# The loads at three stage boundaries in another order, and the down-projection's weight sums on the vector engine alone

## The chip, the cores and the metric

The kernel runs on one core of one Trainium2 chip. The metric is the device time of one execution in microseconds. Five engines work side by side, each through its own list of instructions in order: PE (matrix multiplication), DVE (vector), ACT (scalar), POOL (GpSimd) and SP (which here only issues DMAs). A DMA that SP or POOL issues runs on the 16 DMA engines, and what is queued behind it on its issuer goes on at once unless it has a wait of its own.

## The reference

One decoder layer over 512 tokens with a model width of 2048 and an inner width of 5632, all in float32: sliding-window attention, and then a gated MLP with a causal convolution of width 3 over the positions.

```python
def conv_ffn(h, w_up, conv_w, w_down):
    u = h @ w_up                                             # 512x2048 @ 2048x11264
    up = jnp.pad(u, ((0, 0), (CONV_WIDTH - 1, 0), (0, 0)))
    c = conv_w[0] * up[:, 0:S]
    for j in range(1, CONV_WIDTH):
        c = c + conv_w[j] * up[:, j:j + S]
    gate, val = jnp.split(c, 2, axis=-1)
    return (jax.nn.silu(gate) * val) @ w_down                # 512x5632 @ 5632x2048

h = rms_norm(x, norm_g[0, 0])
m = swa_sink_attention(h, swa_w_in[0], swa_w_out[0], swa_sinks[0], rel_bias_table)
x = x + rms_norm(m, norm_g[0, 1])
h = rms_norm(x, norm_g[0, 2])
x = x + rms_norm(conv_ffn(h, ffn_w_up[0], ffn_conv[0], ffn_w_down[0]), norm_g[0, 3])
```

## The kernel before

Float32 accuracy comes from splitting each operand into a high and a low part: ACT copies the block into the high part (`wh`, line 64), DVE subtracts that from the block for the low part (`wl`, line 65), and each product is three matmuls (`prod`, line 83 records them): high by high, high by low, low by high. Matmuls are issued in program order, and so are the DMAs that go through `in_turn` (line 139, on SP). The order of all other instructions on DVE, ACT and POOL is set by the compiler's scheduler from its own model of time.

The stages are: projections and attention, the output projection, the up-projection, the down-projection. The up-projection works by pairs: for one f, a block of 128 gate columns and 128 value columns for all 512 tokens. f = 0 to 3 are computed in other ways; `up_by_tokens(3)` is the last of these, and its activation forms are computed in a space named `keepers`. Then 40 calls of `up_pair(f)`, f = 4 to 43, follow, counted here as pair 0 to 39. A pair uses seven products in place of eight (a Strassen form): it loads four weight blocks of 512 KB (`b11`, `b21`, `b12`, `b22`, tile `bw`, six buffers), makes four sums of them on DVE (lines 697, 704, 708, 711), splits seven blocks, and multiplies each by a form of the activations, 24 matmuls of 128x256 for one product. DVE also combines the results (lines 715, 717, 719). `gate(f)` then does the convolution (lines 583 to 585) and the gate (590, 592), and stores a tile of `hd` in DRAM through POOL.

The down-projection also uses seven products, of 22 steps over kp, with matmuls of 128x512. Four of them need sums of weight blocks, which are computed ahead and kept in DRAM as `td`: `weight_sums(kp)` loads four blocks of `wdn` of 512 KB into four `ts` tiles, adds on DVE (line 147, four adds) and stores four results through POOL (line 148). `queue_sums(kp)` does the same without DVE: four loads on SP and then four accumulating DMAs on POOL (line 157) and the stores (line 160). The groups kp = 0 to 5 are done within the output projection. The other 16 are done beside the pairs: at every fifth pair (i%5 == 0) a `weight_sums` is begun ahead of the pair's own loads, its adds come in and behind the next pair, and then a `queue_sums` follows. The `ts` tiles (pool `tsu`, four buffers) lie in the space that `keepers` held.

When the last group is done, at i = 36, `tsu` is closed, a tile `hq10` for 16 steps of the first down product's activations is opened in its place, and four fetches of 512 KB from `hd` are issued on SP. The down stage reads its blocks into `raw`, by turns from two pools of two buffers, `wraw` (which the pairs also use) and `wraw2`, which is opened when the up stage is over. `coming` is the list of later fetches; one is issued with every second step of kp.

Of the kernel before, what the change touches and what calls it, by code (L numbers as in the profile page):

```python
# [11 lines left out]
F32 = mybir.dt.float32  # L12
# [6 lines left out]
P = 128  # L19
# [16 lines left out]
NP = NF // 2  # L36
HALF = S // 2
# [4 lines left out]
def trunk(ctx, tc, xT, x, grow, table, onehot, masked, sinks, conv,  # L42
          wkv, wq, wo, wup, wdn, out):
    nc = tc.nc
    pool = lambda name, bufs, **kw: tc.tile_pool(name=name, bufs=bufs, **kw)

    const = ctx.enter_context(pool("const", 1))
    wraw = ctx.enter_context(pool("wraw", 2))
# [8 lines left out]
    def bank(i):  # L57
        return ps.tile([P, 512], F32, name=f"b{i}", bufs=1)
# [4 lines left out]
    def split(hi, lo, src):  # L63
        nc.scalar.activation(hi, src, AF.Copy)  # L64
        nc.vector.tensor_tensor(lo, src, hi.bitcast(F32), ALU.subtract)  # L65

    def halves():
        p = ring["slots"][ring["next"] % len(ring["slots"])]
        ring["next"] += 1
        return p.tile([P, 1024], F32R, name="wh"), p.tile([P, 1024], F32R, name="wl")  # L70
# [67 lines left out]
    def in_turn(o, i):  # L138
        tc.keep_in_program_order(nc.sync.dma_start(o, i))  # L139

    def weight_sums(kp, sums, paced=False):
        t = [sums.tile([P, 1024], F32, name="ts") for _ in range(4)]
        for q in (0, 2, 1, 3):
            (in_turn if paced else nc.gpsimd.dma_start)(t[q], wdn[4 * kp + q])
        yield
        for q, o in ((2, 0), (0, 1), (1, 2), (3, 1)):
            nc.vector.tensor_tensor(t[q], t[q], t[o], ALU.add)
            nc.gpsimd.dma_start(td[kp, :, q, :], t[q])
            yield

    def queue_sums(kp, sums):
        t = [sums.tile([P, 1024], F32, name="ts") for _ in range(4)]
        for q in (2, 0, 1, 3):
            in_turn(t[q], wdn[4 * kp + q])

        def add(q, o):
            nc.gpsimd.dma_start(t[q], o, accum_op=ALU.add)

        def store(q):
            nc.gpsimd.dma_start(td[kp, :, q, :], t[q])  # L160

        add(2, wdn[4 * kp])
        add(0, wdn[4 * kp + 1])
        store(2)
        add(1, t[2])
        store(0)
        add(3, t[1])
        store(1)
        store(3)

    def step(g, n=1):
        for _ in range(n):
            next(g, None)

    with ExitStack() as att:
# [10 lines left out]
        with ExitStack() as ph:  # L186
# [26 lines left out]
            for kt in range(KT):  # L213
                if kt == 0:
                    for h in range(2):
# [3 lines left out]
                        if h == 0:  # L219
                            w = halves()  # L220
                            raw = wraw.tile([P, 1024], F32, name="raw")
# [241 lines left out]
    with ExitStack() as op:  # L463
        sums = op.enter_context(pool("tso", 4))
# [5 lines left out]
        g1 = gp.tile([P, D], F32, name="g1")  # L470
# [63 lines left out]
        for b, bk in enumerate((2, 5, 6, 7)):  # L534
            o = bank(bk)
            for kt in range(KT):
# [3 lines left out]
                if b < 2:  # L540
                    if kt == 0:
                        g = weight_sums(4 + b, sums)
# [23 lines left out]
    batches = [(g, min(g + GB, NP)) for g in range(0, NP, GB)]  # L566
    hq = {}

    def fetch(m, par, g0, g1):
        t, k0 = next((t, k) for t, k, k1 in hq[m, par] if k <= g0 < k1)  # L570
        in_turn(t[:, g0 - k0:g1 - k0, :], hd[m, par, :, g0:g1, :])

    with ExitStack() as us:
# [14 lines left out]
        def gate(f, o):  # L588
            cg = conv_half(o[0], f, 0)
            nc.scalar.activation(cg, cg, AF.Silu)  # L590
            cv = conv_half(o[1], f, 1)
            nc.vector.tensor_tensor(cv, cg, cv, ALU.mult)  # L592
            kp, par = divmod(f, 2)
            nc.gpsimd.dma_start(hd[:, par, :, kp, :].rearrange("m p t -> p m t"),  # L594
                              cv.rearrange("p (m t) -> p m t", m=2))
# [71 lines left out]
        tsu = ExitStack()  # L667
        sums = tsu.enter_context(pool("tsu", 4, side="right"))

        def block(f, r, c):  # L670
            t = bw.tile([P, 1024], F32, name="bw")
            in_turn(t, wup[4 * f + 2 * c + r])
            return t

        def form(t):
            w = halves()
            split(*w, t)
            return w

        def times(o, n, w, fresh):  # L680
            o3 = o[:, :HALF].rearrange("p (a b) -> p a b", a=2)
            a = forms[n]
            for k in range(8):
                prod(o3, cols(w, k), tuple(v[:, :, k, :] for v in a), fresh and k == 0, k == 7, not fresh)

        def shot(o, name):
            t = un.tile([P, HALF], F32, name=name)
            nc.scalar.activation(t, o[:, :HALF], AF.Copy)  # L688
            return t

        def up_pair(f, g):
            X, Y, Z = (bank(k) for k in ((0, 1, 6), (3, 4, 7))[f % 2])
            ug = un.tile([P, S], F32, name="ug", bufs=2)
            uv = un.tile([P, S], F32, name="uv", bufs=2)
            b11, b21 = block(f, 0, 0), block(f, 1, 0)
            t = wraw.tile([P, 1024], F32, name="raw")
            nc.vector.tensor_tensor(t, b11, b21, ALU.add)  # L697
            times(X, 2, form(t), True)
            s1 = shot(X, "s1")
            step(g)  # L700
            b12 = block(f, 0, 1)
            times(Z, 7, form(b12), True)
            s7 = shot(Z, "s7")
            nc.vector.tensor_tensor(t, t, b12, ALU.add)
            times(X, 5, form(t), False)
            s2 = shot(X, "s2")
            step(g)
            nc.vector.tensor_tensor(b11, b11, b12, ALU.add)  # L708
            times(Z, 6, form(b11), False)
            b22 = block(f, 1, 1)  # L710
            nc.vector.tensor_tensor(t, t, b22, ALU.add)
            times(X, 3, form(t), False)
            s3 = shot(X, "s3")
            step(g)
            nc.vector.tensor_tensor(ug[:, :HALF], Z[:, :HALF], s2, ALU.subtract)
            times(Y, 1, form(b21), True)
            nc.vector.tensor_tensor(uv[:, :HALF], s3, s7, ALU.subtract)
            times(X, 4, form(b22), False)
            nc.vector.tensor_tensor(ug[:, HALF:], s1, Y[:, :HALF], ALU.subtract)
            nc.scalar.activation(uv[:, HALF:], X[:, :HALF], AF.Copy, scale=-1.0)  # L720
            gate(f, (ug, uv))

        kp = 6
        for f in range(4, NF):
            i = f - 4
            if i % 5 == 0 and kp < NP:
                work = weight_sums(kp, sums, True)
                step(work)
                kp += 1
            up_pair(f, work if i % 5 == 1 else iter(()))  # L730
            if i % 5 == 1:
                step(work)
            if i % 5 == 1 and kp < NP:
                queue_sums(kp, sums)
                kp += 1
            if kp == NP and tsu:
                tsu.close()
                tsu = None
                early = ctx.enter_context(pool("early", 1, side="right"))
                hq[1, 0] = [(early.tile([P, 16, HALF], F32, name="hq10"), 0, 16)]  # L740
                for g0, g1 in batches[:4]:
                    fetch(1, 0, g0, g1)


    acts.close()
# [3 lines left out]
    y = acc.tile([P, NT, D], F32, name="y")  # L749
    g3 = acc.tile([P, D], F32, name="g3")  # L750
    rest = ctx.enter_context(pool("rest", 1))
    hq[1, 0].append((rest.tile([P, NP - 16, HALF], F32, name="hq10b"), 16, NP))
    raws = (wraw, ctx.enter_context(pool("wraw2", 2)))
    for m, par in ((0, 1), (1, 1)):
        hq[m, par] = [(rest.tile([P, NP, HALF], F32, name=f"hq{m}{par}"), 0, NP)]
    small = ctx.enter_context(pool("small3", 4))
    last = ctx.enter_context(ExitStack())
    hq[0, 0] = [(last.enter_context(pool("hq00", 1)).tile([P, NP, HALF], F32, name="hq00"), 0, NP)]
    coming = [(1, 0, *g) for g in batches[4:]] + [(*q, *g) for q in ((0, 0), (0, 1), (1, 1)) for g in batches]
    nc.scalar.dma_start(g3, grow[2:3, :].to_broadcast([P, D]))  # L760

    XB, ZB = (3, 4, 6, 7), (0, 1, 2, 5)
# [16 lines left out]
        return hi, lo  # L779

    def weight_form(src, kp):
        raw = raws[kp % 2].tile([P, 1024], F32, name="raw")
        table, q = src
        in_turn(raw, td[kp, :, q, :] if table else wdn[4 * kp + q])
        hi, lo = halves()
        split(hi, lo, raw)
        return hi, lo
# [5 lines left out]
    def product(o, form, src, fresh, tail=0):  # L793
        kept = []
        for g0, g1 in batches:
            af = act_form(*form, g0, g1)
            for kp in range(g0, g1):
                wf = weight_form(src, kp)
                if coming and kp % 2 == 0:
                    fetch(*coming.pop(0))  # L800
                if kp >= NP - tail:
                    kept.append((kp, af, g0, wf))
                    continue
                for t in range(2):
                    for e in range(2):
                        multiply(o, kp, af, g0, wf, t, e, fresh)
        return kept
# [13 lines left out]
    sums = {}  # L821
# [23 lines left out]
    product(z_, (a11, a21, 1), (0, 1), True)  # L845
    keep(x_, 1, 0)
    product(x_, (a12, a21, 1), (1, 1), False)
    keep(z_, 0, 1)
    product(z_, (a12, a11, -1), (1, 0), False)
# [93 lines left out]
```

## Time and profile before

| | us |
|---|---|
| median of 3 runs | 1907.91 (1906.57 to 1908.58) |
| the profiled execution | 1905.1 |
| its span | 1903.1 |
| PE busy | 1859.6 (98%) |
| DVE busy | 1456.7 (77%) |
| ACT busy | 982.3 (52%) |
| POOL busy | 124.0 (7%) |

The profile is of one execution, and its times count from the start of the span. An instruction's row gives its start, its duration, the engine and line, the tile that it writes and those that it reads, and in brackets the time that the engine stood idle before it and what released it. `DMA bw<-in_wup` as a releaser is the landing of that transfer. The starts of successive matmuls lie closer together than their durations, since matmuls are pipelined. The granted clock is the share of TensorE's full clock, where 1.00 is 2.4 GHz and 0.50 is 1.2 GHz.

### The profile page before, as it was taken

Reading aid. Unit: us, or ns where it says so; the run is one execution under the profiler, and the core shown is the slowest. Engines: PE = TensorE matmul, PEld = TensorE weight load, DVE = VectorE, ACT = ScalarE, POOL = GpSimd, SP = SyncE. Lnnn points to the kernel's source line nnn. Section 1 sums busy time; section 2 is a strip of 40 time slices with the busy share of each in tenths; the row PEclk is TensorE's granted clock in tenths of the full one; section 3 lists DMA queues with packets and bytes.
Section 4 is the critical chain, followed back from the end, with each engine's and each line's share of the span. In section 5 each row is a group of like instructions: output and inputs, shape, how many; then the busy total and the mean of one; then the engine's idle time right before and its main releaser. Section 6 shows DMA issues by size and latency. Waiting matters only on the chain.

```text
span 1903.1 us, 30165 instructions
## 1 busy us (share of the span) xinstructions
PE 1859.6 (98%) x11822; PEld 1688.7 (89%) x11822; DVE 1456.7 (77%) x2047; ACT 982.3 (52%) x1566; POOL 124.0 (7%) x196
## 2 busy tenths in 40 slices
PE   9999999999999599999999999999998999999998
PEld 7888888888899599999999999999997888888886
DVE  5468888754787689898989898989875666666875
ACT  6357777622443355555555555555544555545553
POOL 0000000012100111101010101010100000000000
PEclk9999999999999799999999999999998999999999
DMA  9533234499641767667585758575652876575673
GB/s 306 157 98 97 93 119 144 149 348 335 245 166 61 263 190 255 210 228 232 200 249 211 244 202 266 193 242 206 200 208 90 326 275 212 176 245 187 245 249 113
DMA packets 112397, 392.02 MB, mean 206 GB/s; under 512 B 13216, under 2 KB 15488, under 8 KB 110336
## 3 DMA queue, kind: packets, MB, share of 16 engines
q1 hardware_dynamic: 83968, 293.86, 44.8%
q0 software_dynamic: 24256, 87.04, 14.4%
q10 hardware_dynamic: 4032, 9.21, 1.5%
q8 instruction: 92, 1.51, 0.3%
q14 instruction: 49, 0.40, 0.1%
HBM read 309.29 MB, written 72.39 MB: 201 GB/s over the span
## 4 chain that ended last, share of the span: by engine, by line
PE 62%; issue 2%; DMA 1%; DVE 1%; ACT 0%; POOL 0%; DVEq 0%; SPq 0%; ACTq 0%; POOLq 0%
PE b L83 62%; DMA bw<-in_wup 0%; DMA raw<-td 0%; DVE wl L65 0%; DMA hd<-c 0%; DVE x L839 0%; POOL hd L594 0%; DVE raw L697 0%; DVE bw L708 0%; ACT wh L64 0%; ACT junk L828 0%; DVE y L830 0%; DVEq L939 0%; DVE c L592 0%; SPq L139 0%
## 5 line engine op out<-in xcount | busy, mean ns | idle before, releaser
L64 ACT ACTIVATE wh<-raw 128x1024 fp32r<-128x1024 f32 (+1 forms) x371 | 388.9, 1056 | 485.0 <-PE b L83 275.8
L65 DVE TENSOR_TENSOR wl<-raw,wh 128x1024 fp32r<-128x1024 f32 (+1 forms) x371 | 449.6, 1219 | 212.0 <-ACT wh L64 210.6
L83 PE MATMUL b<-ah,wh 128*128 128x256 f32 (+1 forms) x1824 | 563.6, 309 | 18.5 <-ACT wh L64 18.5
L83 PE MATMUL b<-ah,wl 128*128 128x256 f32 (+1 forms) x1824 | 557.2, 305 | 2.6 <-DVE wl L65 2.6
L83 PE MATMUL b<-al,wh 128*128 128x256 f32 (+1 forms) x1824 | 556.3, 305 | 0.4 <-DVE al L65 0.4
L83 PEld LDWEIGHTS b<-ah,wh 128*128 128x128 f32 x1824 | 351.1, 192 | 31.0 <-ACT wh L64 20.4
L83 PEld LDWEIGHTS b<-ah,wl 128*128 128x128 f32 x1824 | 350.6, 192 | 18.3 <-DVE wl L65 3.6
L83 PEld LDWEIGHTS b<-al,wh 128*128 128x128 f32 x1824 | 351.2, 193 | 10.9 <-DVE al L65 0.6
L83 PE MATMUL b<-wh 128*128 128x512 f32 x616 | 241.2, 392 | 6.8 <-ACT wh L64 6.8
L64 ACT ACTIVATE wh<-bw 128x1024 fp32r<-128x1024 f32 x160 | 169.1, 1059 | 147.8 <-PE b L83 144.1
L83 PE MATMUL b<-wl,wh 128*128 128x512 f32 x616 | 241.4, 392 | 1.7 <-DVE wl L65 1.7
L83 PE MATMUL b<-wh,wl 128*128 128x512 f32 x616 | 241.1, 391 | 0.0
L65 DVE TENSOR_TENSOR wl<-bw,wh 128x1024 fp32r<-128x1024 f32 x160 | 194.2, 1218 | 7.6 <-ACT wh L64 6.7
L83 PEld LDWEIGHTS b<-wh 128*128 128x128 f32 x616 | 116.4, 189 | 32.2 <-ACT wh L64 7.8
L83 PEld LDWEIGHTS b<-wl,wh 128*128 128x128 f32 x616 | 116.5, 189 | 26.7 <-DVE wl L65 2.6
L83 PEld LDWEIGHTS b<-wh,wl 128*128 128x128 f32 x616 | 116.5, 189 | 24.1
L83 PE MATMUL b<-wh,ah 128*128 128x512 f32 x320 | 126.5, 395 | 0.0
L83 PE MATMUL b<-wh,al 128*128 128x512 f32 x320 | 124.8, 390 | 0.0
L83 PE MATMUL b<-wl,ah 128*128 128x512 f32 x320 | 124.6, 389 | 0.0
L83 PE MATMUL b<-f6h,wh 128*128 128x256 f32 x320 | 91.4, 286 | 2.6 <-ACT s L688 2.6
L83 PE MATMUL b<-f6l,wh 128*128 128x256 f32 x320 | 91.3, 285 | 0.0
L83 PE MATMUL b<-f6h,wl 128*128 128x256 f32 x320 | 91.2, 285 | 0.0
(165 smaller groups left out, 3031.8 us busy)
## 6 DMA issues: line engine op xcount, KB each, us to landing
bw<-in_wup SPq DMA_DIRECT2D x160, 512.0 KB, 4.4
td<-ts POOLq DMA_DIRECT2D x88, 512.0 KB, 5.4
raw<-td SPq DMA_DIRECT2D x88, 512.0 KB, 5.0
raw<-in_wdn SPq DMA_DIRECT2D x66, 512.0 KB, 4.5
ts<-in_wdn SPq DMA_DIRECT2D x64, 512.0 KB, 6.2
ts<-in_wdn POOLq DMA_DIRECT2D x40, 512.0 KB, 8.4
raw<-in_wq SPq DMA_DIRECT2D x32, 512.0 KB, 3.5
raw<-in_wo SPq DMA_DIRECT2D x32, 512.0 KB, 5.0
```

The lines of the kernel that those rows point to most:

```text
L64: nc.scalar.activation(hi, src, AF.Copy)
L65: nc.vector.tensor_tensor(lo, src, hi.bitcast(F32), ALU.subtract)
L83: tc.keep_in_program_order(nc.tensor.matmul(o, l, r, start=start, stop=stop, skip_group_check=more))
```

## The change

All 16 groups beside the pairs now go through `weight_sums`; `queue_sums` stays in the file and is not called. A group's four loads are issued ahead of the loads of the pairs 1, 3, 5, 7, 9, 11, 13, 16, 18, ..., 28, 31 and 33, and its adds are recorded within and behind the pair after it. Pair 0's loads therefore come first on SP. `tsu` is closed behind the whole loop; `hq10` holds 8 steps in place of 16, two fetches follow it, and `wraw2` is opened beside it. In the down stage the four raw buffers are used in turn, and the fetches that were left over are placed behind raws number 3 to 6, the later ones at every second step as before.

```diff
--- before.py
+++ after.py
@@ -723,23 +723,22 @@
         kp = 6
         for f in range(4, NF):
             i = f - 4
-            if i % 5 == 0 and kp < NP:
+            if i % 15 in (1, 3, 5, 7, 9, 11, 13) and kp < NP:
                 work = weight_sums(kp, sums, True)
                 step(work)
                 kp += 1
-            up_pair(f, work if i % 5 == 1 else iter(()))
-            if i % 5 == 1:
-                step(work)
-            if i % 5 == 1 and kp < NP:
-                queue_sums(kp, sums)
-                kp += 1
-            if kp == NP and tsu:
-                tsu.close()
-                tsu = None
-                early = ctx.enter_context(pool("early", 1, side="right"))
-                hq[1, 0] = [(early.tile([P, 16, HALF], F32, name="hq10"), 0, 16)]
-                for g0, g1 in batches[:4]:
-                    fetch(1, 0, g0, g1)
+                up_pair(f, iter(()))
+            else:
+                up_pair(f, work if i else iter(()))
+                if i:
+                    step(work)
+        assert kp == NP
+        tsu.close()
+        early = ctx.enter_context(pool("early", 1, side="right"))
+        hq[1, 0] = [(early.tile([P, 8, HALF], F32, name="hq10"), 0, 8)]
+        wraw2 = ctx.enter_context(pool("wraw2", 2, side="right"))
+        for g0, g1 in batches[:2]:
+            fetch(1, 0, g0, g1)
 
 
     acts.close()
@@ -749,14 +748,14 @@
     y = acc.tile([P, NT, D], F32, name="y")
     g3 = acc.tile([P, D], F32, name="g3")
     rest = ctx.enter_context(pool("rest", 1))
-    hq[1, 0].append((rest.tile([P, NP - 16, HALF], F32, name="hq10b"), 16, NP))
-    raws = (wraw, ctx.enter_context(pool("wraw2", 2)))
+    hq[1, 0].append((rest.tile([P, NP - 8, HALF], F32, name="hq10b"), 8, NP))
+    raws = {"pools": (wraw, wraw, wraw2, wraw2), "next": 0}
     for m, par in ((0, 1), (1, 1)):
         hq[m, par] = [(rest.tile([P, NP, HALF], F32, name=f"hq{m}{par}"), 0, NP)]
     small = ctx.enter_context(pool("small3", 4))
     last = ctx.enter_context(ExitStack())
     hq[0, 0] = [(last.enter_context(pool("hq00", 1)).tile([P, NP, HALF], F32, name="hq00"), 0, NP)]
-    coming = [(1, 0, *g) for g in batches[4:]] + [(*q, *g) for q in ((0, 0), (0, 1), (1, 1)) for g in batches]
+    coming = [(1, 0, *g) for g in batches[2:]] + [(*q, *g) for q in ((0, 0), (0, 1), (1, 1)) for g in batches]
     nc.scalar.dma_start(g3, grow[2:3, :].to_broadcast([P, D]))
 
     XB, ZB = (3, 4, 6, 7), (0, 1, 2, 5)
@@ -779,7 +778,8 @@
         return hi, lo
 
     def weight_form(src, kp):
-        raw = raws[kp % 2].tile([P, 1024], F32, name="raw")
+        raw = raws["pools"][raws["next"] % 4].tile([P, 1024], F32, name="raw")
+        raws["next"] += 1
         table, q = src
         in_turn(raw, td[kp, :, q, :] if table else wdn[4 * kp + q])
         hi, lo = halves()
@@ -796,7 +796,7 @@
             af = act_form(*form, g0, g1)
             for kp in range(g0, g1):
                 wf = weight_form(src, kp)
-                if coming and kp % 2 == 0:
+                if 3 <= raws["next"] - 1 <= 6 or coming and kp % 2 == 0 and raws["next"] > 7:
                     fetch(*coming.pop(0))
                 if kp >= NP - tail:
                     kept.append((kp, af, g0, wf))
```

On SP, at the start of the pairs, the rows before (`ts` are the blocks to be summed, `bw` those of the pairs):

```order
L77 DMA raw<-in_wup 128x1024 x11
L139 DMA ts<-in_wdn 128x1024 x4
L139 DMA bw<-in_wup 128x1024 x8
L139 DMA ts<-in_wdn 128x1024 x4
L139 DMA bw<-in_wup 128x1024 x12
L139 DMA ts<-in_wdn 128x1024 x4
```

and now:

```order
L77 DMA raw<-in_wup 128x1024 x11
L139 DMA bw<-in_wup 128x1024 x4
L139 DMA ts<-in_wdn 128x1024 x4
L139 DMA bw<-in_wup 128x1024 x8
L139 DMA ts<-in_wdn 128x1024 x4
L139 DMA bw<-in_wup 128x1024 x8
```

The four loads of pair 0 stand first, and the first `ts` loads behind them; from there groups of four `ts` loads stand at every eight blocks.

On DVE, at the same place, the rows before:

```order
L584 SCALAR_TENSOR_TENSOR c_5897<-b_5667,cw,c_5897 128x511
L585 SCALAR_TENSOR_TENSOR c_5897<-b_5667,cw,c_5897 128x510
L592 TENSOR_TENSOR c_5897<-c_5892,c_5897 128x512
L147 TENSOR_TENSOR ts<-ts 128x1024 x4
L697 TENSOR_TENSOR raw<-bw 128x1024
L708 TENSOR_TENSOR bw<-bw 128x1024
L65 TENSOR_TENSOR wl<-raw,wh 128x1024
L65 TENSOR_TENSOR wl<-bw,wh 128x1024
L704 TENSOR_TENSOR raw<-raw,bw 128x1024
L697 TENSOR_TENSOR raw<-bw 128x1024
```

and now:

```order
L584 SCALAR_TENSOR_TENSOR c_5897<-b_5667,cw,c_5897 128x511
L585 SCALAR_TENSOR_TENSOR c_5897<-b_5667,cw,c_5897 128x510
L592 TENSOR_TENSOR c_5897<-c_5892,c_5897 128x512
L697 TENSOR_TENSOR raw<-bw 128x1024
L708 TENSOR_TENSOR bw<-bw 128x1024
L65 TENSOR_TENSOR wl<-raw,wh 128x1024
L65 TENSOR_TENSOR wl<-bw,wh 128x1024
L704 TENSOR_TENSOR raw<-raw,bw 128x1024
L147 TENSOR_TENSOR ts<-ts 128x1024
L65 TENSOR_TENSOR wl<-raw,wh 128x1024
L147 TENSOR_TENSOR ts<-ts 128x1024
```

The four adds (line 147) stood ahead of the first sum of pair 0 (line 697); now the first stands behind line 704 and they alternate with splits.

On SP, at the end of the pairs and the start of the down-projection, before (`hq` and `hq10b` are activations, `raw` the down stage's blocks):

```order
L139 DMA ts<-in_wdn 128x1024 x4
L139 DMA hq_14936<-hd 128x1024 x4
L139 DMA bw<-in_wup 128x1024 x12
L139 DMA raw<-td 128x1024
L139 DMA hq10b<-hd 128x1024
L139 DMA raw<-td 128x1024 x2
L139 DMA hq10b<-hd 128x512
L139 DMA raw<-td 128x1024 x2
```

and now:

```order
L139 DMA ts<-in_wdn 128x1024 x4
L139 DMA bw<-in_wup 128x1024 x4
L139 DMA hq_15647<-hd 128x1024 x2
L139 DMA bw<-in_wup 128x1024 x24
L139 DMA raw<-td 128x1024 x4
L139 DMA hq10b<-hd 128x1024
L139 DMA raw<-td 128x1024
```

The fetches from `hd` stood three pairs before the end and are two in place of four, six pairs before it; four raws stand ahead of the next fetch in place of one.

On DVE, around the third pair's `ug` (line 715), before:

```order
L585 SCALAR_TENSOR_TENSOR c_6389<-uv,cw,c_6389 128x510
L65 TENSOR_TENSOR wl<-bw,wh 128x1024
L592 TENSOR_TENSOR c_6389<-c_6384,c_6389 128x512
L65 TENSOR_TENSOR wl<-raw,wh 128x1024
L697 TENSOR_TENSOR raw<-bw 128x1024
L704 TENSOR_TENSOR raw<-raw,bw 128x1024
L715 TENSOR_TENSOR ug<-b_6415,s_6515 128x256
L65 TENSOR_TENSOR wl<-bw,wh 128x1024
L65 TENSOR_TENSOR wl<-raw,wh 128x1024
```

and now:

```order
L147 TENSOR_TENSOR ts<-ts 128x1024
L584 SCALAR_TENSOR_TENSOR c_6383<-uv,cw,c_6383 128x511
L708 TENSOR_TENSOR bw<-bw 128x1024
L584 SCALAR_TENSOR_TENSOR c_6378<-ug,cw,c_6378 128x511
L711 TENSOR_TENSOR raw<-raw,bw 128x1024
L585 SCALAR_TENSOR_TENSOR c_6383<-uv,cw,c_6383 128x510
L585 SCALAR_TENSOR_TENSOR c_6378<-ug,cw,c_6378 128x510
L715 TENSOR_TENSOR ug<-b_6391,s_6493 128x256
L65 TENSOR_TENSOR wl<-raw,wh 128x1024
```

The `wl` from `raw` for the product that follows stood three rows ahead of line 715 and stands behind it now.

## Rows read from the trace of the kernel before

**Rows 1.** Page: span and instructions; then busy us (share) of each engine.

```profile
span 1903.1 us, 30165 instructions
...
PE 1859.6 (98%) x11822; PEld 1688.7 (89%) x11822; DVE 1456.7 (77%) x2047; ACT 982.3 (52%) x1566; POOL 124.0 (7%) x196
```

**Rows 2.** Windows: stretch; busy us (count) of PE, PEld, DVE, ACT, POOL; granted clock.

```profile
624.00:672.00 48.00, 27.17 (x196) 26.44 (x195) 35.81 (x35) 16.85 (x22) 6.67 (x10) 0.79 0.86 298
...
1392.00:1440.00 48.00, 45.12 (x351) 44.46 (x350) 41.04 (x45) 25.44 (x35) 1.45 (x2) 0.93 0.41 140
...
1440.00:1488.00 48.00, 39.44 (x239) 34.78 (x238) 26.72 (x30) 18.43 (x25) 1.43 (x2) 0.86 0.48 173
...
672.00:1392.00 720.00, 720.00 (x6003) 720.00 (x6002) 635.50 (x700) 375.95 (x532) 83.86 (x123) 1.00 0.68 223
...
1500.00:1860.00 360.00, 360.00 (x1590) 298.06 (x1590) 249.90 (x239) 187.98 (x209) 0.00 (x0) 1.00 0.67 230
...
719.00:742.00 23.00, 23.00 (x194) 23.00 (x193) 23.00 (x26) 11.93 (x18) 2.38 (x5) 1.00 0.69 244
...
720.00:1344.00 624.00, 624.00 (x5203) 624.00 (x5202) 560.56 (x616) 328.27 (x464) 71.76 (x106) 1.00 0.68 223
```

**Rows 3.** Waits of PE and SP: us in total, times, longest.

```profile
PE b L83 <- ACT wh L64: 25.3, 4, 16.4
...
SPq L139 <- DVE al L617: 36.4, 1, 36.4
```

**Rows 4.** Timeline of PE, first seam: start, duration, instruction, idle before.

```profile
640.58 0.58 PE L83 MATMUL b<-ah,wh 128*128 128x256 f32 x1 [16.39 <-ACT wh L64]
...
643.19 0.58 PE L83 MATMUL b<-ah,wl 128*128 128x256 f32 x1 [1.81 <-DVE wl L65]
```

**Rows 5.** Timelines of SP, DVE and ACT, first seam.

```profile
626.56 1.75 SPq L139 DMA_DIRECT2D ts<-in_wdn  x4
...
628.36 3.49 SPq L139 DMA_DIRECT2D bw<-in_wup  x6
...
603.37 1.22 DVE L615 SCALAR_TENSOR_TENSOR f4l<-xf,f4h 128x1024 fp32r<-128x1024 f32 x1
...
628.01 0.69 DVE L592 TENSOR_TENSOR c<-c,c 128x512 f32<-128x512 f32 x1
...
638.22 1.22 DVE L697 TENSOR_TENSOR raw<-bw 128x1024 f32<-128x1024 f32 x1 [1.36 <-DMA bw<-in_wup]
...
639.47 1.06 ACT L64 ACTIVATE wh<-raw 128x1024 fp32r<-128x1024 f32 x1 [13.62 <-DVE raw L697]
```

**Rows 6.** Timeline of PE, second and third seam.

```profile
1397.03 0.53 PE L83 MATMUL b<-ah,wh 128*128 128x256 f32 x1 [2.12 <-ACT wh L64]
...
1464.58 0.50 PE L83 MATMUL b<-wh 128*128 128x512 f32 x1 [2.97 <-ACT wh L64]
...
1475.27 0.79 PE L83 MATMUL b<-wh 128*128 128x512 f32 x1 [3.86 <-ACT wh L64]
```

**Rows 7.** Timeline of SP, second and third seam.

```profile
1383.63 2.60 SPq L139 DMA_DIRECT2D hq<-hd  x4
...
1468.80 0.79 SPq L139 DMA_DIRECT2D raw<-td  x2
```

**Rows 8.** Groups of DVE, 720 to 1344: count, busy us, mean ns, idle before.

```profile
L147 DVE TENSOR_TENSOR ts<-ts 128x1024 f32<-128x1024 f32 x28 | 34.1, 1217 | 1.3 <-DMA ts<-in_wdn 1.3
```

**Rows 9.** Waits of DVE, 720 to 1344.

```profile
DVE wl L65 <- ACT wh L64: 33.2, 50, 1.7
...
DVE raw L697 <- DMA bw<-in_wup: 17.3, 18, 2.1
```

**Rows 10.** Timeline of DVE in a pair.

```profile
761.43 0.42 DVE L715 TENSOR_TENSOR ug<-b,s 128x256 f32<-128x256 f32 x1 [0.75 <-PE b L83]
...
761.77 1.21 DVE L704 TENSOR_TENSOR raw<-raw,bw 128x1024 f32<-128x1024 f32 x1
...
762.90 1.22 DVE L65 TENSOR_TENSOR wl<-bw,wh 128x1024 fp32r<-128x1024 f32 x1
```

## The prediction

> **What bounds the kernel now.** The views were read in this order: the page's head and shares, the windows of equal length along the span, the waits of PE, PE's timeline at the places where it stands, then the timelines of SP, DVE and ACT at the same places, and last DVE's groups and waits between them. The page puts PE at 98% of the span [rows 1]. The windows say where the other part is: between 672 and 1392 us PE is busy for all of 720 us at full clock and does 6003 matmuls, 0.120 us each, while three windows of 48 us, at 624, 1392 and 1440, hold 27.2, 45.1 and 39.4 us of PE and granted clocks of 0.79, 0.93 and 0.86 [rows 2]. These are the three seams: the start of the pairs, the place where the last weight sums make room, and the start of the down-projection. Nearly all of PE's idle time stands behind one wait, ACT's wh [rows 3].
>
> What each seam loses is read from the windows as missing matmuls. At 624: 400 would fit, 196 ran, 204 x 0.120 = 24.5 us, of them 20.8 idle and 3.7 in a lowered clock. At 1392: 400 - 351 = 49, 5.9 us, of them 2.9 idle. At 1440 the shapes are mixed. The up stage ends at 1464.58 - 2.97 = 1461.6 [rows 6]; until then 180 matmuls fit, so 59 of the 239 are 512 wide, at 0.226 us each (360 us for 1590 [rows 2]) worth 13.4 of the 26.4 us left: 13.0 us lost, 8.6 idle and 4.4 in the clock. Together 43.4 us; a reordering of the seams can't give more.
>
> **Seam 1 (the loads of pair 0 go ahead of the ts loads).** PE stops at 640.58 - 16.39 = 624.2 and restarts at half speed at 640.58, to wait another 1.81 us for wl [rows 4]. SP issues the ts loads at 626.56, when the last reader of the space beneath them is done (the wait on al, 36.4 us long), and pair 0's blocks behind them at 628.36 [rows 3, 5]. The blocks' own space was last read by the f4l instruction of 603.37, so in the new order they can start at about 604.6, and even with the 9.9 us that lay between their issue at 628.36 and L697 at 638.22, behind 2 MB of ts loads, they are there at 614.5 [rows 5]. DMA then releases nothing, and what is late next is DVE: its gate of f=3 ends with the L592 at 628.01 + 0.6, and the adds of the ts blocks, which stood ahead of L697, now stand behind it. From L697's start to PE's in before: 638.22, ACT 639.47, PE 640.58, so 2.36 us [rows 4, 5]. New restart: 628.6 + 2.4 = 631.0, idle 6.8. The wl follows L708 on DVE and ends near 632.2, another 1.1 us. For the clock I take 1.9, between 1.0 and the 3.7 of before. The seam then costs 9.8 (8.9 to 11.6): **gain 14.7** (12.9 to 15.6).
>
> **Seam 2 (room for the last fetches).** SP issues four hq fetches at 1383.63, after the last stores of the ts tiles, and the next blocks only behind them; PE stands 2.12 us at 1397.03 [rows 6, 7]. Now the last group of sums begins at pair 33, two fetches stand in front of the blocks of the last six pairs, and the adds are over in pair 34: the stores land about 6 us behind them, before the block buffer that the first load behind the fetches wants is free. No pause is then left: **gain 5.9**, and 0 if the stores are late.
>
> **Seam 3 (raws of the down stage).** PE stands 2.97 us at 1464.58 for the gate of f=43 and again 3.86 us at 1475.27, because raws were loaded only at 1468.80, on SP behind a fetch, into space that the up stage had held to its end [rows 6, 7]. With wraw2 opened on the space of the ts tiles, four raws are there long before the end, and the next fetches stand behind them. The second pause goes, and the first stays, since ACT's and DVE's gate of f=43 still stands ahead of the first split: 2.8 idle, some 1.3 more for wl, and 1.2 to 3.0 of clock, 6.2 in the middle: **gain 6.8** (5.9 to 7.7). The sum of the seams is 27.4.
>
> **The middle (sums on DVE in place of accumulating DMAs).** Eight groups of sums come to DVE, 32 more adds of 1.217 us, 1.137 start to start (761.77 to 762.90 for L704 of the same size) [rows 8, 10]: 36.4 us of work. What goes is work of POOL and of the DMA queues, which are not waited for (DMA share 0.68 [rows 2]): worth nothing by itself. The cover is DVE's idle time. Between 720 and 1344 us it is busy 560.6 of 624; less 28 adds of 1.137 that is 17.1 us for each of 30.95 pairs. Two pairs with one group in them are 2 x 17.1 + 4.55 = 38.7 of 40.3 us, 96%. The idle of before is mostly not needed: 33.2 of its 63.4 us is wl waiting for wh, that is DVE at the heels of ACT, which waits for PE; 17.3 is L697 waiting for blocks [rows 9]. And behind a group of adds at 719 DVE ran 23.0 of 23 us without a pause while PE missed nothing [rows 2]. So I take it to fit, with one place that can't: in pair 2, DVE has L715 ahead of the wl of the next product. L715 reads the product that PE has just ended (in another pair it waited for PE at 761.43, and the next instruction starts 0.34 later [rows 10]), then comes the wl of 1.2: 1.6 us in which PE has a single matmul to do. With a clock loss of as much as 1, and 0.9 for smaller pauses where a wl is only two products ahead, the middle costs 3.5 (0 to 12).
>
> The sum: -14.7 - 5.9 - 6.8 + 3.5 = -23.9. Against the profiled execution's 1905.1 (a span of 1903.1 and 2.0 around it [rows 1]) 1881.2; that execution lies 2.8 under the median of the runs, so **1884.0** for the median.
>
> **The rivals.**
> (a) *DVE keeps its waits and becomes the bound.* Between 720 and 1344 some 30 more adds are 34.1 us. If the whole idle time of before stays, because each wait is really for a landing or for wh in its own turn, all of it is lost, 36 us over the 33 pairs with sums: 1905.1 - 27.4 + 36 = 1913.7, median 1916.5. It is slower than before from the point where less than 9 of the 36 us find room in the idle time. For it: DVE at 96%, and on SP the loads of blocks queue behind ts loads that wait for the stores of the group before. Against: the 23 us without a pause. Chance 0.06.
> (b) *Small pauses that cost clock.* If the short lead makes PE stand 1.6 us in each of the 16 two-pair stretches, and each pause costs as much again (at 1392 it was 2.9 idle and 3.0 clock), the middle costs 51: 1905.1 - 27.4 + 51, median 1931.5. Even half of that is no gain. For it: that ratio [rows 2], and that it stood for only 2.12 us at a stretch there [rows 6]. Against: elsewhere the order leaves the lead as it was or by two products. Chance 0.05. The Trainium skill (TensorE: Matmul & The Clock Gate, "A second HAM failure mode: psum-queue depth-cycling") tells of just this: PE idling briefly between groups of matmuls often enough for its clock to swing, with throughput lost though each matmul is as fast as before. By that rule the change is no gain; the trace agrees that a pause costs clock, and shows no repeated ones yet.
> (c) *Only the first seam gains.* If the two fetches hold up the blocks of pair 34 and the raws still come late, -14.7 + 3.5: 1893.9, median 1896.7. For it: the fetch waits for stores, as in before. Against: everything behind it has a whole pair of lead. Chance 0.17.
> (d) *No loss in the middle.* 1905.1 - 27.4, median 1880.5. Chance 0.15.
> (e) *The scheduler's order undoes it*, the blocks waiting for space as the ts loads did: within a few us of before. For it: a tile's space is known by its pool alone; against: the reader of 603.37. Chance 0.05.
>
> **The numbers.** My forecast has a chance of 0.52. The range of 1877 to 1899 takes in (c) and (d) and leaves out (a), (b) and (e), 0.16. Runs of this kernel can't tell less than 0.2%, 3.8 us, from no change: faster 0.52 + 0.17 + 0.15 and a bit of the rest, 0.86; same 0.04; slower 0.10.
>
> **What would show it.** Right: in the windows of the changed kernel, the one at 624 with some 320 of 400 matmuls; PE restarting near 631 behind ACT's wh, SP's blocks issued near 604; no pause near the end of pair 34; one pause, not two, behind the up stage; DVE over 0.94 busy in the pairs, PE with one pause in pair 2. Wrong: PE waits for wl or wh in many pairs, a granted clock under 1.00 in windows between 700 and 1350, L697 waiting longer than 2 us for blocks, or a second pause at the last seam.

## The result and the profile after

The changed kernel takes 1879.97 us (median of 4, 1879.19 to 1881.47) where the kernel before takes 1907.55 in the same comparison: a ratio of 0.9856, with an interval of 0.9839 to 0.9873. The forecast was 1884.0, in a range of 1877 to 1899. The profiled execution took 1879.95 us, 25.2 less than that of before.

The page of the changed kernel, its span and its busy times, to be read against [rows 1]:

```profile
span 1878.2 us, 30119 instructions
...
PE 1853.1 (99%) x11822; PEld 1684.0 (90%) x11822; DVE 1485.2 (79%) x2079; ACT 978.8 (52%) x1566; POOL 95.1 (5%) x164
```

PE does the same number of matmuls and is now busy for 99% of a shorter span. DVE is busy for 28.5 us more, POOL for 28.9 less.

The windows of the changed kernel, with the columns of [rows 2]:

```profile
624.00:672.00 48.00, 41.08 (x318) 40.78 (x319) 46.16 (x48) 21.98 (x30) 4.71 (x8) 0.89 0.73 263
...
672.00:1392.00 720.00, 717.43 (x5977) 717.03 (x5976) 671.05 (x738) 377.11 (x537) 57.77 (x94) 1.00 0.58 204
...
1392.00:1440.00 48.00, 48.00 (x402) 48.00 (x402) 34.63 (x39) 22.76 (x33) 1.44 (x2) 1.00 0.28 89
...
1440.00:1488.00 48.00, 44.05 (x196) 36.33 (x196) 32.54 (x30) 24.78 (x26) 0.71 (x1) 0.93 0.82 300
...
720.00:1344.00 624.00, 622.92 (x5191) 622.71 (x5191) 585.04 (x645) 326.58 (x464) 51.44 (x84) 1.00 0.60 208
```

The first window holds 318 matmuls where it held 196, the third 402 where it held 351, at a clock of 1.00. The one between 672 and 1392, full before, has lost 2.6 us of PE and 26 matmuls. DVE went from 560.6 to 585.0 of the 624 us between 720 and 1344, 0.938 of them.

All pauses of PE of over 0.3 us behind 600 us, from its timeline, to be read against [rows 4, 6] and the first line here, a pause of the kernel before in pair 0:

```profile
655.88 0.38 PE L83 MATMUL b<-f6h,wh 128*128 128x256 f32 x1 [2.62 <-ACT s L688]
```

```profile
630.41 0.58 PE L83 MATMUL b<-ah,wh 128*128 128x256 f32 x1 [6.80 <-ACT wh L64]
...
631.72 0.58 PE L83 MATMUL b<-ah,wl 128*128 128x256 f32 x1 [0.51 <-DVE wl L65]
...
687.57 0.39 PE L83 MATMUL b<-ah,wl 128*128 128x256 f32 x1 [1.48 <-DVE wl L65]
...
786.59 0.39 PE L83 MATMUL b<-f6h,wh 128*128 128x256 f32 x1 [1.08 <-ACT s L688]
...
1446.45 0.79 PE L83 MATMUL b<-wh 128*128 128x512 f32 x1 [2.98 <-ACT wh L64]
...
1448.22 0.80 PE L83 MATMUL b<-wl,wh 128*128 128x512 f32 x1 [0.98 <-DVE wl L65]
```

At the first seam they are 6.8 and 0.5 us long where they were 16.4 and 1.8, and a third, the 2.62 us at 655.88 that complete the 20.8 idle there, is gone. The pause at 1397 is gone, and of the two behind the up stage the second. New are the one at 687.57 and one at 786.59. The loads behind the first, on SP, and the end of the gate and the first sum on DVE:

```profile
604.04 1.75 SPq L139 DMA_DIRECT2D bw<-in_wup  x4
...
625.99 1.75 SPq L139 DMA_DIRECT2D ts<-in_wdn  x4
```

```profile
627.44 0.69 DVE L592 TENSOR_TENSOR c<-c,c 128x512 f32<-128x512 f32 x1
...
628.05 1.22 DVE L697 TENSOR_TENSOR raw<-bw 128x1024 f32<-128x1024 f32 x1
...
633.85 1.22 DVE L147 TENSOR_TENSOR ts<-ts 128x1024 f32<-128x1024 f32 x1
```

Pair 0's blocks are issued at 604.04, as soon as the last reader of their space is through, and 22 us ahead of the ts loads [rows 5]. L697 follows L592 with nothing between, and the first add (L147) comes behind L704. At the last seam SP's rows are:

```profile
1405.53 21.58 SPq L139 DMA_DIRECT2D raw<-td  x4
...
1450.27 0.32 SPq L139 DMA_DIRECT2D hq10b<-hd  x1
...
1450.68 0.38 SPq L139 DMA_DIRECT2D raw<-td  x1
```

Four raws are issued between 1405 and 1427, and the fifth at 1450.68, behind a fetch.

### The profile page after: what moved, and what is told of

Same layout as the page of the kernel before. It is cut to its first block, busy times and chain, and to the rows that moved or that the text cites. A ratio compares the mean times of both kernels' runs of the same rounds, so it can differ in the third digit from the quotient of the medians.

```text
span 1878.2 us, 30119 instructions
## 1 busy us (share of the span) xinstructions
PE 1853.1 (99%) x11822; PEld 1684.0 (90%) x11822; DVE 1485.2 (79%) x2079; ACT 978.8 (52%) x1566; POOL 95.1 (5%) x164
## 4 chain that ended last, share of the span: by engine, by line
PE 97%; DVE 1%; DMA 1%; issue 0%; ACT 0%; SPq 0%; DVEq 0%; ACTq 0%
PE b L83 95%; PE b L86 2%; DVE wl L65 0%; DMA raw<-in_wkv 0%; DMA bw<-in_wup 0%; DVE raw L697 0%; DVE bw L708 0%; ACT wh L64 0%; DVE x L839 0%; DVE x L625 0%; DVE c L585 0%; DVE c L584 0%; DVE raw L711 0%; ACT ah L613 0%; DVE ug L715 0%
## 5 line engine op out<-in xcount | busy, mean ns | idle before, releaser
L688 ACT ACTIVATE s<-b 128x256 f32<-128x256 f32 x160 | 60.2, 376 | 159.0 <-PE b L83 157.8
L147 DVE TENSOR_TENSOR ts<-ts 128x1024 f32<-128x1024 f32 x88 | 107.2, 1218 | 20.0 <-DMA ts<-in_wdn 19.5
```

## The experiments

Each comparison has its own runs of the kernel before, whose median lay between 1905.6 and 1907.6; the changed kernel's 1880.0 is from the first comparison. The edits are shortened: a remark behind a # stands for lines left out, or for another variant. No experiment takes the second seam by itself, or the move of the sums from accumulating DMAs to DVE; for these the account rests on the traces of before and after.

**The first seam undone.** The first group of the changed kernel begins ahead of pair 0.

```diff
-            if i % 15 in (1, 3, 5, 7, 9, 11, 13) and kp < NP:
+            if (i == 0 or i % 15 in (3, 5, 7, 9, 11, 13) or i % 15 == 1 and i > 1) and kp < NP:
```

> The changed kernel, but the first group's ts loads go ahead of pair 0's blocks again; nothing else differs. Theory (each seam costs its own pause, and the pauses add): PE restarts near 640 us again behind ACT's wh, after 16 us of idle, and 14.6 us come back: about 1894.5 us. Rival (the gain at the first seam comes from the whole pipeline being less loaded by accumulating DMAs, not from the order of two loads): the pause stays near 7 us and the time within 4 us of 1880.

Measured: 1891.8 us, 11.8 more than the changed kernel. PE's pause at the seam and its window of the pairs:

```profile
640.52 0.58 PE L83 MATMUL b<-ah,wh 128*128 128x256 f32 x1 [16.30 <-ACT wh L64]
...
672.00:1392.00 720.00, 719.89 (x5999) 719.64 (x5998) 671.43 (x739) 377.09 (x535) 58.89 (x96) 1.00 0.60 207
```

The pause is back to within 0.1 us, and so is the third one (2.34 us at 655.99), so both hang on the order of those two loads. It costs 2.8 less than expected, and 2.6 of that is the window between 672 and 1392, which is all but full again (5999 matmuls, not 5977). The pause in pair 2 goes with DVE's order: here the `wl` from `raw` stands ahead of pair 2's L715 (699.07 and 700.98), as in the kernel before. Whether that order comes from the loads or from the first group's adds, which this edit also moves one pair earlier, was not separated.

**The first seam alone.** The kernel before, with its accumulating DMAs, and only its first group moved behind pair 0's loads (the `queue_sums` that follows it moves one pair with it).

```diff
-            if i % 5 == 0 and kp < NP:
+            if (i == 1 or i and i % 5 == 0) and kp < NP:
```

> The kernel before, with accumulating DMAs and all, but its first group of sums begins ahead of pair 1 and not of pair 0. Theory: the first seam's 14.6 us go and nothing else: about 1893 us, with both later pauses (2.1 and 3.9 us) in place. Rival (the order helps only with the lighter DMA traffic of the changed kernel): within 4 us of 1907.5.

Measured: 1893.0 us against 1907.1, a ratio of 0.9925 (0.9900 to 0.9949). PE's pauses at the three seams:

```profile
630.66 0.58 PE L83 MATMUL b<-ah,wh 128*128 128x256 f32 x1 [6.80 <-ACT wh L64]
...
1383.06 0.39 PE L83 MATMUL b<-ah,wh 128*128 128x256 f32 x1 [1.81 <-ACT wh L64]
...
1460.52 0.79 PE L83 MATMUL b<-wh 128*128 128x512 f32 x1 [3.66 <-ACT wh L64]
```

The first is that of the changed kernel, and the other two stand nearly as before (2.12 and 3.86 us there). About half of the change's gain is one transposition of two sets of loads; the sums' engine has no part in it.

**The last seam undone.**

```diff
-        wraw2 = ctx.enter_context(pool("wraw2", 2, side="right"))
-    raws = {"pools": (wraw, wraw, wraw2, wraw2), "next": 0}
+    raws = (wraw, ctx.enter_context(pool("wraw2", 2)))
-                if 3 <= raws["next"] - 1 <= 6 or coming and kp % 2 == 0 and raws["next"] > 7:
+                if coming and kp % 2 == 0:
```

> The changed kernel, but the down stage reads its blocks as before: wraw2 opened only behind the up stage, two raws by parity of the step, fetches at even steps from the first. Theory: the second pause of about 4 us behind the up stage comes back with its lowered clock, 6.6 us: about 1886.6 us. Rival (the pause went because the fetches became fewer and earlier, whatever the raws do): within 2 us of 1880.

Measured: 1888.2 us, 8.2 more. The second pause of PE behind the up stage, and a row of DVE in the pairs, of which more below:

```profile
1457.50 0.80 PE L83 MATMUL b<-wh 128*128 128x512 f32 x1 [3.57 <-ACT wh L64]
```

```profile
777.81 1.23 DVE L697 TENSOR_TENSOR raw<-bw 128x1024 f32<-128x1024 f32 x1 [0.29 <-DMA bw<-in_wup]
```

The second is back, though the fetches are as many as in the changed kernel and the first two as early, so the rival falls. On SP one raw is issued at 1406.18 and the next two at 1451.30, behind a fetch of 1450.92. The edit undoes two things, the four buffers and the place of the fetches, and they were not separated.

**No adds.** The sums that the down stage reads are not computed in this kernel; loads and stores stay.

```diff
-            nc.vector.tensor_tensor(t[q], t[q], t[o], ALU.add)
+            if not paced:
+                nc.vector.tensor_tensor(t[q], t[q], t[o], ALU.add)
```

> The changed kernel without the 64 adds on DVE beside the pairs (the sums that the down stage reads are then not computed; loads and stores stay). Theory (DVE has room for them except at two places): PE's pauses in the third pair (1.5 us) and near 786 us (1.1 us) go, 3.2 us with the clock: about 1877 us. Rival (the adds cost more than shows, since DVE at 94% delays the splits all along): more than 6 us, below 1874.

Measured: 1876.4 us, 3.6 less, near the 3.2 expected. The window of the pairs is full again:

```profile
672.00:1392.00 720.00, 720.00 (x6003) 720.00 (x6002) 616.18 (x681) 381.92 (x538) 56.63 (x92) 1.00 0.57 203
```

So 64 adds, some 73 us at 1.137 each (61.5 by the busy times of the two pages, 1485.2 and 1423.7), cost the kernel under 4 us, of which the two pauses are 26 x 0.120 = 3.1.

**One, two and four operations more in each group.** An operation on a ts tile that changes nothing, behind one, two or all four of the adds.

```diff
             nc.vector.tensor_tensor(t[q], t[q], t[o], ALU.add)
+            for _ in range(int(paced and q == 1)):     # q in (0, 3) for two, all for four
+                nc.vector.tensor_tensor(t[q], t[q], t[q], ALU.max)
```

> The changed kernel with one more DVE operation per group of sums (the maximum of a ts tile with itself, 128x1024, about 1.14 us), so five in place of four in two pairs. DVE is busy for 471.9 of the 500 us between 800 and 1300 us, so two pairs of 40.3 us have 2.3 us of room. Theory (what counts is whether DVE's work fits into the time of two pairs): it fits, 0 to 3 us more than 1880. Rival (what counts is the lead of each split, which is only two products in every second pair, so every operation more delays PE): 1.1 us for each of 16 groups, 18 us more, about 1898.

> The same with two more operations per group: 2.27 us in two pairs against 2.3 us of room. Theory: on the edge, 0 to 12 us more than 1880, first pauses with lowered clock. Rival: 36 us more, about 1916.

> The same with four more operations per group, eight in two pairs: 4.55 us against 2.3 us of room. Theory: DVE is the bound and 2.3 us are lost in each of some 15 stretches of two pairs, 34 us, with some clock on top: 1914 to 1935 us. Rival (a split's lead): 73 us more, about 1953.

Measured: 1883.3, 1900.3 and 1928.7 us, which is 3.3, 20.3 and 48.7 more than without. The first comes out just past the edge of what the theory of room had (0 to 3) and the last within it, the second between the two theories, so neither is right there. The windows of the one with one more operation:

```profile
672.00:1392.00 720.00, 717.50 (x5973) 716.69 (x5972) 689.75 (x756) 375.88 (x537) 58.92 (x96) 1.00 0.58 205
```

and of the one with two more, between 672 and 1392 and just behind two of its pauses:

```profile
672.00:1392.00 720.00, 703.36 (x5820) 700.39 (x5819) 690.26 (x753) 365.80 (x521) 57.55 (x94) 1.00 0.57 201
...
690.00:693.00 3.00, 2.48 (x14) 2.48 (x15) 3.00 (x4) 1.94 (x3) 0.00 (x0) 0.72 0.54 190
...
773.00:776.00 3.00, 1.61 (x13) 1.61 (x14) 3.00 (x4) 2.46 (x4) 0.39 (x1) 1.00 0.44 175
```

The trace of the first is of an execution of 1879.6 us, the fastest of its four (the others took 1883.2 to 1884.6), so it doesn't show where the 3.3 us lie. DVE is busy for the same 690 of 720 us in both, 96%, and PE stands for 2.5 us in the one and 16.6 in the other. DVE's busy share doesn't tell the two apart. PE's waits do, and with them DVE's order at one of them (the waits in us in total, times and longest, over the whole execution; the program has two lines more, so L717 is the subtraction of L715):

```profile
PE b L83 <- DVE wl L65: 17.9, 13, 2.3
```

```profile
772.78 0.42 DVE L717 TENSOR_TENSOR ug<-b,s 128x256 f32<-128x256 f32 x1 [0.33 <-PE b L83]
...
773.12 1.22 DVE L65 TENSOR_TENSOR wl<-raw,wh 128x1024 fp32r<-128x1024 f32 x1
```

At 774.39 PE stands for 1.48 us, as it does at nine places: DVE has the `ug` subtraction, which waits for PE, ahead of the `wl` that PE needs next. It is the pause of pair 2 again, and the compiler's order now has it all along the pairs. With four more operations a second kind grows, the copies on ACT being late, while most pauses are still of the first kind. A time within the range does therefore not show that the theory's reason is right. PE's waits there:

```profile
PE b L83 <- DVE wl L65: 24.3, 19, 2.4
...
PE b L83 <- ACT s L690: 11.5, 10, 2.9
```

**The gate of f=3 behind pair 0's first products.** The first sum and splits of pair 0 are hoisted, that is recorded ahead of the last activation form, and the gate is recorded behind pair 0's third product.

```diff
+        def begin(f):          # loads b11, b21, b12; first sum; two splits
+        o3, pre = up_by_tokens(3, lambda: begin(4))
-            gate(f, o)
+            return o, pre
             times(X, 5, form(t), False)
+            if late:
+                late()         # gate(3, o3)
```

> The changed kernel, but pair 0's first three loads, its first two splits and the sum ahead of them are recorded ahead of the last activation form and of the gate of f=3, and that gate behind pair 0's third product. Theory (what holds the first seam now is that DVE and ACT do the gate of f=3 ahead of the first split, which waits for PE's end, while the blocks are there 13 us before): the pause of 6.8 us and the half clock after it go, 10 us: about 1870 us. Rival (the split is late for another reason, a free tile or the settling of the last form): the pause stays over 4 us, above 1875.

Measured: 1873.6 us, a ratio of 0.9823 (0.9808 to 0.9838) to the kernel before. The first split on DVE:

```profile
614.29 1.22 DVE L65 TENSOR_TENSOR wl<-raw,wh 128x1024 fp32r<-128x1024 f32 x1
```

The split is ready by 615.5, some 8 us before PE needs it, and there is no pause at the seam. Of the expected 10 us, 6.4 are seen; three pauses came in the pairs behind it. Their cause was argued, not shown: DVE has the gate, the sums and the first group's adds together there.

```profile
651.45 0.38 PE L83 MATMUL b<-f5h,wl 128*128 128x256 f32 x1 [1.22 <-DVE wl L65]
...
678.56 0.38 PE L83 MATMUL b<-ah,wh 128*128 128x256 f32 x1 [1.17 <-ACT wh L64]
...
679.82 0.39 PE L83 MATMUL b<-ah,wl 128*128 128x256 f32 x1 [0.76 <-DVE wl L65]
```

**The first splits of the down stage ahead of the gate of f=43.** `wraw2`, `hq10` and its two fetches are recorded ahead of the last pair for this.

```diff
+        def down_ahead():
+            down.append(act_form((1, 0), None, -1, *batches[0]))
+            down.extend(weight_form((1, 2), k) for k in range(3))
+            if end:
+                end()          # down_ahead, in the last pair
             gate(f, (ug, uv))
```

> The changed kernel, but the first activation form and the first three splits of the down stage are recorded ahead of the gate of f=43. Theory (what holds the last seam is that gate alone): the pauses of 3.0 and 1.0 us and the half clock go, 6.6 us: about 1873.5 us. Rival (the blocks are behind, and the next raws, which land 9 us after the end of the up stage, hold PE a little later): a pause moves to the fifth block, gain under 3 us.

Measured: 1879.6 us, no gain. The rival was right. PE's pauses:

```profile
1446.44 0.50 PE L83 MATMUL b<-wh 128*128 128x512 f32 x1 [0.47 <-ACT uv L720]
...
1459.88 0.50 PE L83 MATMUL b<-wh 128*128 128x512 f32 x1 [2.25 <-ACT wh L64]
```

The pause of 3 us at the seam is 0.5, and a new one stands 13 us later. ACT's row ahead of it and SP's at the fifth raw:

```profile
1458.78 1.06 ACT L64 ACTIVATE wh<-raw 128x1024 fp32r<-128x1024 f32 x1 [8.20 <-DMA raw<-td]
```

```profile
1452.73 0.32 SPq L139 DMA_DIRECT2D hq10b<-hd  x1
...
1453.10 0.42 SPq L139 DMA_DIRECT2D raw<-td  x1
```

ACT waits 8.2 us for a raw that SP issued at 1453.10, behind a fetch that was itself issued only at 1452.73.

**Both.**

> Both of these edits together. Theory (the two seams have nothing to do with each other): the gains add, 16.6 us: about 1863.5 us. Rival: one of the pauses only moves, and the time is that of the better of the two, about 1870.

Measured: 1870.2 us (0.9810, 0.9795 to 0.9824), the rival's time, though 3.4 less than the first edit by itself took. PE's idle time behind the up stage is 3.1 us (0.47, 1.87 and 0.77) where it is 4.2 with the first edit alone (2.97 and 1.27); the second edit moves most of its pause and takes little of it away. The window between 672 and 1392 has 18 matmuls more than there (5981 and 5963), where the two kernels do not differ.

**Both, with the fetches three raws later, and then with the groups one pair later.**

```diff
-                elif 3 <= raws["next"] - 1 <= 6 or coming and kp % 2 == 0 and raws["next"] > 7:
+                elif 6 <= raws["next"] - 1 <= 9 or coming and kp % 2 == 0 and raws["next"] > 10:
```

```diff
-            if i % 15 in (1, 3, 5, 7, 9, 11, 13) and kp < NP:
+            if i and (i - 1) % 15 in (1, 3, 5, 7, 9, 11, 13) and kp < NP:
```

> The kernel with both hoists, and the first four fetches of the down stage placed behind raws number 7 to 10 in place of 4 to 7. In the trace with both hoists ACT waits 7.8 us for the fifth raw, which SP issues behind a fetch into space that the last store of the gate still reads. Theory (the pause that moved to the fifth block is this fetch's wait on SP): raws number 5 to 7 are issued as their buffers come free, PE's pauses of 1.9 and 0.8 us some 13 us behind the seam go with their clock, and about 4.5 us are gained on 1870.2: about 1865.5 us. Rival (the fifth block's slot for the split parts is what comes late): the pause stays, within 1.5 us of 1870.

> The same, and every group of sums beside the pairs begun one pair later (2, 4, ..., 14, 17, ...). With both hoists DVE has the first group's adds, the gate of f=3 and pair 0's sums together, and PE pauses for 1.2, 1.2 and 0.8 us between 650 and 680 us. Theory (these pauses are the debt of that heap on DVE): they go, 3 us on the one before: about 1862.5 us. Rival (the pauses come from the compiler's order wherever a group stands and only move): within 1 us of the one before.

Measured: 1867.2 us (0.9799, 0.9784 to 0.9813) and 1863.2 (0.9777, 0.9763 to 0.9790). SP at the end of the up stage, in the first of them:

```profile
1398.26 37.22 SPq L139 DMA_DIRECT2D raw<-td  x7
...
1442.57 0.32 SPq L139 DMA_DIRECT2D hq10b<-hd  x1
```

Seven raws are issued ahead of the fetch, and of the pauses behind the up stage only 0.5 us is left. That the pause went is the trace's evidence; the times alone (3.0 us by the medians, 2.1 by the ratios, whose intervals overlap) would not show it. With the groups one pair later, 4.0 us less in the same comparison, the three pauses between 650 and 680 us become two of 0.7 and 0.6. The window of the pairs of that kernel:

```profile
672.00:1392.00 720.00, 719.07 (x5991) 718.67 (x5990) 674.30 (x742) 377.44 (x537) 58.92 (x96) 1.00 0.59 207
```

It is 42.4 us under the kernel before and 16.7 under the changed one, both by medians (the second across two comparisons; some 15 by the ratios); PE's pauses behind 600 us are 2.1 us in all.

## Why the prediction was right

**The bound and the seams.** The mechanism was right at each seam, and each term was read again by the matmuls missing from a window. The first seam now loses 82 x 0.120 = 9.8 us, and 0.4 more ahead of the window, as PE came to the end of f=3 0.6 us earlier; 14.3 gained, where 14.7 was forecast. PE restarts at 630.41, forecast 631.0; the blocks are issued at 604.04, forecast 604.6; what is late next is DVE, on which L697 follows L592 at once. Two `al` of the last activation form stand ahead of the gate there (L617, at 623.30 and 624.74), and the first hoist, which takes the pause away, goes ahead of both, so the gate alone was not tested. The pause of 2.62 us at 655.88 had no term in the prediction, which put nearly all idle time down to ACT's wh: that is 25.3 of the 32.3 us at the three seams, wl being 4.3 and this pause the rest. That it went is part of the gain, and the prediction gave no reason for it; there it was lucky. The second seam's 5.9 are gained whole; the two fetches now stand at 1286.19 on SP, and no pause follows them. At the last, the up stage ends at 1443.5; 29 of the window's 196 matmuls are before it and 167 of 0.226 us fill 37.8 of 44.5 us, so 6.7 are lost where 13.0 were: 6.3 gained, forecast 6.8.

**The middle.** Forecast 3.5, measured 26 x 0.120 = 3.1. DVE's busy time rose by 28.5 us, where 36.4 of work were forecast, and its share came to 0.938, just under the 0.94 named as a sign. The pause in pair 2 was forecast as 1.6 us from the order of L715 and wl, and it is 1.48 at 687.57. DVE's rows just ahead of it:

```profile
685.96 0.42 DVE L715 TENSOR_TENSOR ug<-b,s 128x256 f32<-128x256 f32 x1 [1.82 <-PE b L83]
...
686.30 1.22 DVE L65 TENSOR_TENSOR wl<-raw,wh 128x1024 fp32r<-128x1024 f32 x1
```

The second pause was not foreseen in its place. L697 waited 1.88 us for a block at 777.51, the split behind the sum came late on ACT, and the copy of a product, queued behind three splits, came later still, where PE wanted the bank:

```profile
777.51 1.23 DVE L697 TENSOR_TENSOR raw<-bw 128x1024 f32<-128x1024 f32 x1 [1.88 <-DMA bw<-in_wup]
...
783.31 1.06 ACT L64 ACTIVATE wh<-raw 128x1024 fp32r<-128x1024 f32 x1 [3.14 <-DVE raw L711]
...
786.17 0.36 ACT L688 ACTIVATE s<-b 128x256 f32<-128x256 f32 x1
```

It hangs on that landing: in the kernel with the last seam undone DVE and ACT have the same order here, L697 waits 0.29 us (the row at 777.81 above), and PE has no such pause. The 0.9 us that the prediction set aside was for pauses of another kind, so that the sum of the middle fits is in part luck.

The granted clock between 672 and 1392 is 1.00, so the clock term of the middle was nothing; what is lost beyond the 2.6 us of idle is seen in the starts of the matmuls around the pause at 687.57:

```profile
685.80 0.28 PE L83 MATMUL b<-al,wh 128*128 128x256 f32 x1
...
687.79 0.28 PE L83 MATMUL b<-ah,wh 128*128 128x256 f32 x1
```

Elsewhere a start follows the last one after 0.12 us. Here 685.80, 687.57 and 687.79 leave 1.77 and 0.22, which is 1.75 us more than two such steps, for a pause that the profile gives as 1.48: some 0.27 us are lost with the pause at full clock.

**The size.** The terms sum to 23.4 us gained, the two profiled executions differ by 25.2; 0.6 of the rest lies ahead of the first seam, 0.2 outside the span (2.0 us before, 1.8 now), and about 1.0 was not traced. The larger part of the 4 us between 1884.0 and 1879.97 is the step from execution to median: 2.8 us were added because the profiled execution of before lay that far under its median, and that of the changed kernel lies at its median (1879.95 and 1879.97). That was one draw of a scatter (the runs of before went from 1903.4 to 1913.3), not a property of the kernel.

**The clock's terms were too small.** At the first seam 1.9 us were taken and 10.2 - 7.3 idle = 2.9 measured; at the last 2.1 and 6.7 - 4.0 = 2.7. At the first seam less idle time than forecast (7.3, not 7.9) made up for part of it. One execution does not size such a term: with the same 7.3 us of idle the window at 624 holds 323 matmuls in the trace with one more operation and 313 in the one without adds, so 1.9 and 3.1 us beyond the idle time.

```profile
624.00:672.00 48.00, 40.69 (x323) 40.19 (x323) 45.61 (x46) 22.46 (x31) 3.77 (x7) 0.93 0.68 246
...
624.00:672.00 48.00, 40.69 (x313) 40.19 (x312) 40.57 (x42) 24.85 (x32) 5.75 (x10) 0.89 0.76 282
```

**The rivals.** (a) fell: the idle time of DVE took 24.5 us more of work between 720 and 1344, its wait for blocks went from 17.3 us [rows 9] to 4.2, and the kernel without adds gains 3.6 us. Nearest to it is the kernel with four more operations for each group, 48.7 us slower, but there too most of PE's pauses are of the kind of pair 2. (b) fell for this change. Small repeated pauses are what the kernel with two more operations has: 157 matmuls fewer than in the changed kernel between 672 and 1392, 18.8 us, for 14.1 us more of idle, so a third on top and not as much again. By the 0.27 us above, some 2.7 of these 4.7 us go with the ten more pauses at any clock, which leaves some 2 for the lowered clock behind one of them. (c) and (e) fell, the one by the missing pauses at 1397 and 1475, the other by the blocks' issue at 604.04. (d) gave 1880.5, nearest to the median, but its reason was wrong: the middle did lose 3.1 us.

## What to carry to other kernels

At the boundary of two stages, look at what each queue holds in front of the first transfer that the next stage needs: a load that waits for space holds up the loads behind it on its queue (here the ts loads of 626.56 held pair 0's blocks until 628.36), and putting it behind them gave about half of the gain here. When a pause goes, read which engine's queue is late next, and move the piece that PE waits for ahead of the piece that it doesn't, all the way to the next buffer: the hoist at the last seam by itself gained nothing, because its pause moved 13 us on to a block that a fetch held up. Where an engine is filled to 96%, its busy share doesn't tell whether PE stalls; look in the order for an instruction that waits for PE ahead of one that PE waits for.

## What was not expected of the hardware

The clock did not answer to all pauses alike. Behind the pause of 1.48 us at 774.39 in the kernel with two more operations the granted clock was 1.00 (2.4 GHz), and 0.72 behind its 2.33 us at 690.52, with 0.50 (1.2 GHz) from 692 to 694 (the rows of 773 and 690 above). In the kernel before, three pauses of 2.1 to 3.9 us at the later seams, with shorter ones behind them, cost 3.0 and 4.4 us beyond their idle time, and the granted clock was 0.50 from 1398 to 1402 and from 1466 to 1478.
